# Splitting the weights of an encoder trunk into two float32r parts by DMAs of GpSimd instead of by VectorE

## The chip, the cores and the metric

One core of a Trainium2 chip runs the whole program. The metric is the device time of one execution in microseconds (us). The engines are named as in the profile: PE (TensorE matmuls), PEld (its weight loads), DVE (VectorE), ACT (ScalarE), POOL (GpSimd) and SP (SyncE, which here only issues DMAs).

## The reference

Two layers of an encoder over 512 tokens of width 1024, in float32. Each layer has a token mixer and a gated MLP, each between two RMS norms and added to the residual:

```python
for l in range(DEPTH):
    xn = rms_norm(x, norm_pre_mix[l])
    mix = mixer_layer(xn, w_in[l], w_out[l], ...)
    x = x + rms_norm(mix, norm_post_mix[l])
    xn = rms_norm(x, norm_pre_ffn[l])
    ff = conv_ffn(xn, w_up[l], conv_w[l], conv_b[l], w_down[l])
    x = x + rms_norm(ff, norm_post_ffn[l])
```

The mixer projects `xn` by `w_in` (1024 x 3584) into the inputs of three mixers, dilated window attention (A), a gated linear recurrence (B) and differential attention (C), and projects their outputs by `w_out` (1024 x 1024). `conv_ffn` projects to 2 x 2816 columns (`w_up`), mixes each column over three neighbouring tokens, multiplies `silu(gate) * val`, and projects back (`w_down`).

## The kernel before, in words

**Two-part products.** TensorE works on float32r, a float32 with a rounded mantissa. To keep float32's accuracy, an operand `a` of the large projections is kept as a rounded part `hi` and a rest `lo = a - hi`, both float32r, and a product is three matmuls: hi x hi, hi x lo, lo x hi (`prod`). So each weight tile is needed in both parts.

**Weight tiles.** `lay_weights` cuts all weights of a layer into 104 tiles of 128 partitions x 1024 float32 (512 KB). The tiles of `hg0` and `hg1` use only 768 columns (384 KB). `weight` (line 518) records what loads and splits a tile: SP loads it into `raw` (3 buffers), a copy rounds it into `hi`, and VectorE subtracts, `lo = raw - hi`. `hi` and `lo` have 5 buffers each (`WB`, line 1182), plus one pair for the last tile of a layer's MLP (`V_TILE`). The copy may go to VectorE or to ScalarE, as the planner decides (`copy`, line 241). In all 228 tiles are loaded: the 208 of two layers and, once more, the 6 tiles of `hg0` and `ib` and the first 4 of the MLP in each layer, because those projections run over half of the tokens at a time.

**Stages of a layer.** The norm transposes `xn` to the feature-major layout. `mixer` runs its projections and attention pieces in the order of `STEPS` (line 111), first `hg0` and `ib` twice over 256 tokens each (matmuls of 256 columns). Of an `hg0` tile such a half uses 18 matmuls (2 k-tiles, 3 outputs, 3 products), of an `ib` tile 24. Then come the output projection (first halves of the columns for all tokens, then second halves token block by token block, with four tiles held), and the MLP. The MLP starts with two column groups over 256 tokens at a time, 8 tile loads with 24 matmuls of 256 columns each; after that an up tile is used by 24 matmuls of 512 columns, and so is a down tile. For the last three pairs of down tiles all six tiles are held and the four token blocks run through them, six matmuls of 512 columns for each tile and token block.

**What sets the order.** The program is recorded op by op, and `Plan.order` (line 334) decides the order on every engine by a list schedule over estimated costs: each engine in turn takes the ready op of the lowest priority number. `weight` records its ops 1500 places ahead (`AHEAD`, line 109), so that a weight is loaded as soon as a buffer is free. A buffer is free when its last reader is done. The engines then execute these orders strictly, each waiting on semaphores. In that schedule a DMA issued by SP costs 1 ns for 350 bytes, and whoever needs its data comes 2000 ns later (`LAG["dma"]`). Besides SP's loads there are few other queues: GpSimd does 24 + 16 `memset`s and 48 power instructions (`pow`, the reciprocal roots of the norms; `row_rstd` and `rstd`), and no DMA. Everything that the planner issues has one line in the profile, L499.

## Time and profile before

| what | value |
|---|---|
| median of 3 runs | 1433.16 us (1432.78 to 1433.42) |
| the profiled execution's own time | 1432.73 us |
| its span, first to last instruction | 1431.0 us |
| TensorE matmuls, busy | 1391.2 us, 97% |
| VectorE, busy | 1051.7 us, 73% |
| ScalarE, busy | 656.6 us, 46% |
| GpSimd, busy | 56.7 us, 4% |
| mean granted TensorE clock | 0.999 |
| read from HBM | 128.4 MB, 93 GB/s over the span with what is written |

Busy time of an engine counts its instructions, not its waits. A row of the table of stretches gives, for each engine, the busy microseconds in it and the number of instructions, then the granted clock of TensorE (1.00 is full), the mean busy share of the core's 16 DMA engines, and what they moved. In groups of instructions, `128x1024 fp32r<-128x1024 f32` is the shape and type written and read, `x204` the count, then come the total busy time, the mean of one in ns, and the idle time of that engine just before these instructions with what ended it. `rounded` is the arena of float32r buffers (`hi` and `lo` parts), `full` that of float32 buffers, `w_d` the weights in HBM, `bank` a PSUM bank.

### The profile page before, as it was taken

What the parts mean: (1) busy time and instruction counts of PE and PEld (TensorE: products, weight loads), DVE (VectorE), ACT (ScalarE), POOL (GpSimd) and SP (SyncE); (2) the same over time, 40 slices, a digit from 0 to 9 for tenths busy, and PEclk for the clock granted to TensorE, in tenths of its full rate; (3) what the DMA queues carried; (4) which work ended last, traced back from release to release, by engine and by line L of the source; (5) the groups of instructions that cost most, each with busy time, mean ns of one, the idle gap of its engine ahead of it and who ended that gap; (6) DMA issues with size and microseconds to landing.
All of it is one profiled execution on the core that took longest, in us unless ns stands there. A gap on an engine that the chain in (4) does not pass through costs nothing.

```text
span 1431.0 us, 20879 instructions
## 1 busy us (share of the span) xinstructions
PE 1391.2 (97%) x8128; PEld 1208.8 (84%) x8128; DVE 1051.7 (73%) x1905; ACT 656.6 (46%) x1201; POOL 56.7 (4%) x94
## 2 busy tenths in 40 slices
PE   6999999999999999999999999999999999999998
PEld 6998888978888888888899888898788888888886
DVE  7779999886976546655777899888688765565574
ACT  5746886564533122213367478856555321321131
POOL 2000000001000000000010000000010000000000
PEclk9999999999999999999999999999999999999999
DMA  7412111221632223232262121012224223222321
GB/s 257 140 66 76 49 42 33 75 88 60 198 101 100 99 93 103 89 103 89 77 217 90 62 77 41 31 63 89 74 88 163 94 97 103 89 103 90 102 74 59
DMA packets 39363, 133.92 MB, mean 94 GB/s; under 512 B 5088, under 2 KB 5600, under 8 KB 39264
## 3 DMA queue, kind: packets, MB, share of 16 engines
q1 hardware_dynamic: 39264, 132.59, 27.5%
q8 instruction: 64, 1.05, 0.3%
q14 instruction: 35, 0.29, 0.1%
HBM read 128.37 MB, written 4.19 MB: 93 GB/s over the span
## 4 chain that ended last, share of the span: by engine, by line
PE 75%; DVE 17%; ACT 3%; issue 3%; DMA 1%; POOL 0%; DVEq 0%; SPq 0%; POOLq 0%; ACTq 0%
PE bank L499 75%; DVE full L499 10%; DVE rounded L499 6%; DVE qz L499 2%; ACT full L499 1%; ACT rounded L499 1%; DMA full<-w_d 1%; POOL full L499 0%; ACT L499 0%; DMA full<-x_d 0%; SPq L499 0%; DVEq L1245 0%; DVE masks L499 0%; POOLq L1245 0%; DVEq L499 0%
## 5 line engine op out<-in xcount | busy, mean ns | idle before, releaser
L499 PE MATMUL bank<-rounded 128*128 128x512 f32 (+1 forms) x6480 | 1234.5, 347 | 6.0 <-ACT full L499 2.0
L499 PEld LDWEIGHTS bank<-rounded 128*128 128x128 f32 x6480 | 1032.2, 190 | 153.5 <-DVE full L499 4.3
L499 DVE TENSOR_TENSOR rounded<-full,rounded 128x1024 fp32r<-128x1024 f32 (+2 forms) x276 | 302.0, 1106 | 50.9 <-ACT rounded L499 43.1
L499 ACT ACTIVATE rounded<-full 128x1024 fp32r<-128x1024 f32 (+2 forms) x162 | 152.8, 947 | 234.8 <-PE bank L499 182.7
L499 ACT ACTIVATE full<-bank,full 128x512 f32<-128x512 f32 (+1 forms) x184 | 122.7, 671 | 276.4 <-PE bank L499 243.0
L499 ACT ACTIVATE full<-full 128x512 f32<-128x512 f32 (+7 forms) x302 | 167.9, 572 | 168.0 <-DVE full L499 155.4
L499 DVE CAST rounded<-full 128x1024 fp32r<-128x1024 f32 (+1 forms) x114 | 74.2, 651 | 153.4 <-PE bank L499 147.5
L499 DVE SCALAR_TENSOR_TENSOR full<-bank,full 128x511 f32<-128x511 f32 x176 | 130.4, 748 | 55.4 <-ACT full L499 52.7
L499 DVE TENSOR_TENSOR full<-full 128x512 f32<-128x512 f32 (+2 forms) x277 | 145.7, 545 | 9.5 <-ACT full L499 3.2
L499 ACT ACTIVATE full<-bank 128x512 f32<-128x512 f32 (+3 forms) x188 | 103.2, 562 | 49.4 <-PE bank L499 37.1
L499 PE MATMUL bank<-ident,full 128*128 128x128 f32 x560 | 90.0, 281 | 18.9 <-DVE full L499 18.5
L499 PEld LDWEIGHTS bank<-ident,full 128*128 128x128 f32 x560 | 65.7, 143 | 33.8 <-DVE full L499 23.5
L499 PE MATMUL bank<-full 128*128 128x128 f32 (+2 forms) x640 | 83.5, 299 | 2.2 <-ACT full L499 1.4
L499 PEld LDWEIGHTS bank<-full 128*128 128x128 f32 (+1 forms) x640 | 70.6, 180 | 13.5 <-ACT full L499 5.0
L499 DVE SCALAR_TENSOR_TENSOR full<-full 128x512 f32<-128x512 f32 x96 | 69.6, 747 | 11.0 <-POOL full L499 10.4
L499 ACT ACTIVATE rounded<-bank 64x256 fp32r<-64x256 f32 (+1 forms) x148 | 63.3, 430 | 28.2 <-PE bank L499 21.0
L499 PE MATMUL bank<-qz,full 128*128 128x128 f32 x448 | 66.0, 288 | 5.8 <-DVE full L499 5.6
L499 POOL TENSOR_TENSOR full<-full,half 128x1 f32<-128x1 f32 (+1 forms) x48 | 42.1, 878 | 719.0 <-DVE full L499 719.0
L499 PEld LDWEIGHTS bank<-qz,full 128*128 128x128 f32 x448 | 56.1, 190 | 14.0 <-DVE full L499 11.9
L499 DVE TENSOR_TENSOR full<-bank,full 128x512 f32<-128x512 f32 (+1 forms) x56 | 35.9, 649 | 21.8 <-PE bank L499 21.5
L499 DVE TENSOR_TENSOR qz<-full 64x256 f32<-64x256 f32 x112 | 46.6, 416 | 4.4 <-PE bank L499 2.5
L499 DVE TENSOR_TENSOR rounded<-bank,rounded 64x256 fp32r<-64x256 f32 (+1 forms) x84 | 44.3, 535 | 5.4 <-ACT rounded L499 4.5
(54 smaller groups left out, 365.0 us busy)
## 6 DMA issues: line engine op xcount, KB each, us to landing
full<-w_d SPq DMA_DIRECT2D x204, 512.0 KB, 3.3
full<-w_d SPq DMA_DIRECT2D x24, 384.0 KB, 3.4
full<-x_d SPq DMA_DIRECT2D x8, 512.0 KB, 5.0
full<-gains_d SPq DMA_DIRECT2D x8, 512.0 KB, 4.1
spill<-full SPq DMA_DIRECT2D x4, 512.0 KB, 2.7
full<-spill SPq DMA_DIRECT2D x4, 512.0 KB, 4.2
out_d<-full SPq DMA_DIRECT2D x8, 256.0 KB, 2.0
abias<-abias_d SPq DMA_DIRECT2D x1, 448.0 KB, 7.1
```

What stands on the lines that cost most here:

```text
L499: f(*[real(v) for v in op.args], **{k: real(v) for k, v in op.kw.items()})
```

## The change

From the ninth tile on, a weight is no longer loaded raw. GpSimd issues a DMA from HBM straight into `hi`, whose type is float32r, so that the DMA rounds; a copy writes `lo = -hi` (on VectorE or ScalarE); and a second DMA of GpSimd reads the same weights from HBM once more and adds them to `lo`. The first 8 tiles (6 of 768 columns, 2 of 1024) are loaded and split as before. The planner's estimates follow: a DMA issued by GpSimd keeps GpSimd for 1000 ns (`SOFT`), and the lag of 2000 ns holds for every DMA.

```diff
+SOFT = 1000.0
+FIRST = 8
...
-        if op.eng == "gpsimd":
+        if op.eng == "gpsimd" and op.method != "dma_start":
...
-        lag = lambda a, b: LAG["dma"] if a.eng == "sync" else LAG[a.eng] if a.eng == b.eng else LAG["other"]
+        lag = lambda a, b: LAG["dma"] if a.method == "dma_start" else LAG[a.eng] if a.eng == b.eng else LAG["other"]
...
-            if e == "sync":
-                free[e] = max(t + 50, t + op.cost)
-                op.end = t + op.cost
+            if op.method == "dma_start":
+                issue = 50 if e == "sync" else SOFT
+                free[e] = max(t + issue, t + op.cost * (e == "sync"))
+                op.end = t + issue * (e != "sync") + op.cost
...
         with nc.ahead(AHEAD):
-            raw = self.t([128, n], "raw")
-            nc.sync.dma_start(raw, self.a["w"][l, index, :, 0:n])
+            src = self.a["w"][l, index, :, 0:n]
+            self.loads += 1
+            if self.loads <= FIRST:
+                raw = self.t([128, n], "raw")
+                nc.sync.dma_start(raw, src)
             hi = self.t([128, n], tag + "hi", F32R)
-            nc.copy(hi, raw)
+            if self.loads <= FIRST:
+                nc.copy(hi, raw)
+            else:
+                nc.gpsimd.dma_start(hi, src)
             lo = self.t([128, n], tag + "lo", F32R)
-            nc.vector.tensor_tensor(lo, raw, hi.bitcast(F32), op=ALU.subtract)
+            if self.loads <= FIRST:
+                nc.vector.tensor_tensor(lo, raw, hi.bitcast(F32), op=ALU.subtract)
+            else:
+                nc.copy(lo, hi.bitcast(F32), -1.0)
+                nc.gpsimd.dma_start(lo, src, accum_op=ALU.add)
         return hi, lo
```

Since the planner sorts anew, the order changes on every engine. Two places on GpSimd and one on VectorE follow. A row names the line, the operation, what it writes and reads, and in brackets the semaphores that it waits for: of the DMAs, those that wait for `PE` are rounding DMAs (a `hi` buffer has to be free), those that wait for `DVE` or `Activation` are adding DMAs (the negated copy has to be there). `DMASW0` to `DMASW7` are the semaphores of GpSimd's DMAs: each DMA also waits for the one eight places before it.

GpSimd from the output projection to the start of the MLP in layer 0; `full<-full,half` are the power instructions of the norms. Before:

```order
L499 TENSOR_TENSOR full<-full,half 128x4 [waits DVE_49,Activation_49,Pool_49]
L499 TENSOR_TENSOR full<-full,half 128x1 [waits DVE_49] x7
L499 TENSOR_TENSOR full<-full,half 128x1 [waits DVE_49,Pool_49]
L499 MEMSET full 64x4 [waits DVE_49,Activation_49]
```

Now:

```order
L502 TENSOR_TENSOR full<-full,half 128x1 [waits DVE_49]
L502 DMA rounded<-w_d 128x1024 [waits DMASW1_49,DVE_49]
L502 TENSOR_TENSOR full<-full,half 128x1 [waits DVE_49] x3
L502 DMA rounded<-w_d 128x1024 [waits DMASW2_49,PE_49]
L502 TENSOR_TENSOR full<-full,half 128x1 [waits DVE_49]
L502 DMA rounded<-w_d 128x1024 [waits DMASW3_49,PE_49]
L502 DMA rounded<-w_d 128x1024 [waits DMASW4_49,PE_49]
L502 DMA rounded<-w_d 128x1024 [waits DMASW6_49,DMASW5_49,PE_49]
L502 DMA rounded<-w_d 128x1024 [waits Activation_49]
L502 TENSOR_TENSOR full<-full,half 128x1 [waits DVE_49]
L502 DMA rounded<-w_d 128x1024 [waits DMASW7_49,DVE_49]
```

The power instructions, which stood in a row, now stand behind DMAs that wait for buffers and for negated copies.

GpSimd inside the MLP of layer 0, where it had nothing to do before (the loads were a run on SP, `L499 DMA full<-w_d 128x1024 x61`). Now:

```order
L502 DMA rounded<-w_d 128x1024 [waits DMASW2_49,PE_49]
L502 DMA rounded<-w_d 128x1024 [waits DMASW3_49,PE_49]
L502 DMA rounded<-w_d 128x1024 [waits DMASW4_49,DVE_49]
L502 DMA rounded<-w_d 128x1024 [waits DMASW5_49,PE_49]
L502 DMA rounded<-w_d 128x1024 [waits DMASW6_49,Activation_49]
L502 DMA rounded<-w_d 128x1024 [waits DMASW7_49,PE_49,Activation_49]
```

Rounding and adding DMAs alternate in one queue: two that wait for TensorE, then an adding one, and the next rounding one behind it.

VectorE in the MLP of layer 0: the taps of the convolution (`SCALAR_TENSOR_TENSOR`), the product with the gate, the split of its result (128x512), and of the weights (128x1024). Before:

```order
L499 CAST rounded<-full 128x512
L499 TENSOR_TENSOR rounded<-full,rounded 128x512 x2
L499 TENSOR_TENSOR rounded<-full,rounded 128x1024
L499 CAST rounded<-full 128x1024
L499 TENSOR_TENSOR rounded<-full,rounded 128x1024
L499 SCALAR_TENSOR_TENSOR full<-bank_66,full 128x511 x2
L499 CAST rounded<-full 128x1024
L499 TENSOR_TENSOR rounded<-full,rounded 128x1024
```

Now:

```order
L502 SCALAR_TENSOR_TENSOR full<-bank_66,full 128x511 x2
L502 TENSOR_TENSOR full<-full 128x512
L502 TENSOR_SCALAR rounded<-rounded 128x1024 x2
L502 SCALAR_TENSOR_TENSOR full<-bank_65,full 128x511 x2
L502 SCALAR_TENSOR_TENSOR full<-bank_63,full 128x511 x2
L502 TENSOR_TENSOR full<-full 128x512
L502 TENSOR_SCALAR rounded<-rounded 128x1024 x2
```

The subtractions of 1024 columns are gone; negating copies (`TENSOR_SCALAR`) stand where rounding copies (`CAST`) stood. Over the program GpSimd now issues 440 DMAs, SP 220 loads fewer.

## Rows read from the trace of the kernel before

**Rows 1.** The page's head: busy time, share of the span, instructions of each engine.

```profile
span 1431.0 us, 20879 instructions
...
PE 1391.2 (97%) x8128; PEld 1208.8 (84%) x8128; DVE 1051.7 (73%) x1905; ACT 656.6 (46%) x1201; POOL 56.7 (4%) x94
```

**Rows 2.** Table of stretches (starts of layers and MLPs, mixers, inner MLP).

```profile
core 0: us, PE busy (x) PEld busy (x) DVE busy (x) ACT busy (x) POOL busy (x), PEclk, DMA share, GB/s
29.00:58.00 29.00, 29.00 (x244) 29.00 (x243) 21.85 (x41) 22.23 (x32) 0.00 (x0) 1.00 0.58 195
100.00:200.00 100.00, 96.16 (x690) 85.70 (x689) 93.33 (x238) 73.89 (x134) 3.70 (x8) 1.00 0.16 54
200.00:300.00 100.00, 97.96 (x717) 88.31 (x715) 89.97 (x217) 65.99 (x152) 5.77 (x8) 1.00 0.21 70
371.00:394.00 23.00, 23.00 (x145) 20.95 (x146) 20.52 (x26) 12.96 (x17) 0.00 (x0) 1.00 0.60 200
500.00:600.00 100.00, 100.00 (x442) 82.75 (x441) 57.94 (x73) 25.74 (x36) 0.00 (x0) 1.00 0.29 100
724.00:753.00 29.00, 27.66 (x232) 27.46 (x232) 21.59 (x28) 19.53 (x30) 2.64 (x4) 1.00 0.65 217
800.00:900.00 100.00, 95.90 (x686) 86.27 (x687) 94.69 (x243) 74.20 (x134) 3.37 (x7) 1.00 0.16 54
900.00:1000.00 100.00, 97.88 (x726) 87.95 (x725) 88.66 (x215) 66.08 (x150) 6.11 (x8) 1.00 0.20 65
1075.00:1098.00 23.00, 22.68 (x144) 20.58 (x144) 20.36 (x26) 13.46 (x17) 0.00 (x0) 1.00 0.58 189
```

**Rows 3.** Waits, whole span: who waited for whom; us in total, times, longest.

```profile
PEld bank L499 <- DVE full L499: 42.6, 75, 7.3
...
PE bank L499 <- DVE full L499: 26.2, 36, 7.3
ACT rounded L499 <- DMA full<-w_d: 16.2, 13, 4.2
```

**Rows 4.** Groups of instructions, each shape apart: subtractions and rounding copies of weights.

```profile
L499 DVE TENSOR_TENSOR rounded<-full,rounded 128x1024 fp32r<-128x1024 f32 x204 | 249.3, 1223 | 32.8 <-ACT rounded L499 25.1 <-DVE rounded L499 0.5
...
L499 ACT ACTIVATE rounded<-full 128x1024 fp32r<-128x1024 f32 x108 | 114.1, 1058 | 89.5 <-PE bank L499 77.5 <-DMA full<-w_d 11.9
...
L499 DVE CAST rounded<-full 128x1024 fp32r<-128x1024 f32 x96 | 66.5, 693 | 121.5 <-PE bank L499 115.7 <-DMA full<-w_d 1.6
...
L499 DVE TENSOR_TENSOR rounded<-full,rounded 128x768 fp32r<-128x768 f32 x24 | 22.7, 951 | 9.7 <-ACT rounded L499 9.7
...
L499 ACT ACTIVATE rounded<-full 128x768 fp32r<-128x768 f32 x24 | 20.2, 843 | 26.1 <-PE bank L499 21.6 <-DMA full<-w_d 4.3
```

**Rows 5.** DMA queue and issues (KB each, median us to landing); SP's issue of weights.

```profile
q1 hardware_dynamic: 39264, 132.59, 27.5%
...
full<-w_d SPq DMA_DIRECT2D x204, 512.0 KB, 3.3
full<-w_d SPq DMA_DIRECT2D x24, 384.0 KB, 3.4
full<-x_d SPq DMA_DIRECT2D x8, 512.0 KB, 5.0
...
L499 SPq DMA_DIRECT2D full<-w_d x228: 327/328/600, 3.1 to 1383.2; - x114
...
DMA to landing us min/median/max: 2.8/3.3/9.1
```

**Rows 6.** Groups of instructions: GpSimd's power instruction of the norms.

```profile
L499 POOL TENSOR_TENSOR full<-full,half 128x1 f32<-128x1 f32 x32 | 26.0, 812 | 464.8 <-DVE full L499 464.8
```

**Rows 7.** TensorE in order of time, start of layer 0: start, length, operation.

```profile
14.64 2.73 PE L499 MATMUL bank<-rounded 128*128 128x256 f32 x12
...
29.01 41.16 PE L499 MATMUL bank<-rounded 128*128 128x256 f32 x341
```

More of the change, by code (lines that the diff above doesn't have):

```diff
@@ L504, in __init__ @@
         self.nc, self.const, self.a = plan, const, a
+        self.loads = 0
     def t(self, shape, tag, dt=F32):
```

## The prediction

> **What bounds the kernel now.** I read the page's head first [rows 1]: TensorE is busy for 97% of the span, VectorE for 73%, GpSimd for 4%. So the question is not how much VectorE work goes, but where TensorE stands still for VectorE. The table of stretches [rows 2] answers that. Through the gated MLP TensorE is busy without a gap (500 to 600 us: 442 matmuls, 226 ns each), while VectorE is at 58%: nothing can be won there. TensorE has gaps only in the two token-mixing stages, where VectorE is at 89 to 95%: 3.84 and 2.04 us in layer 0, 4.10 and 2.12 us in layer 1, 12.1 us in all. The waits say the same [rows 3]: TensorE's two rows on VectorE come to 68.8 us, but they count weight loads beside matmuls, and only gaps in the matmul column move the end. Weights are hardly waited for: 16.2 us of ScalarE's time, none of TensorE's.
>
> The same table shows where the DMAs are dense: at the starts of the layers and of the MLPs 256-column matmuls use up a weight tile in half the time, and there the 16 DMA engines are busy for 58 to 65% of the stretch, against 29% inside the MLP.
>
> **The change, part by part.** The sum is made against the profiled execution, 1432.7 us, 0.4 us under the median of the runs.
>
> *VectorE loses its subtractions.* Of 228 tiles the first 8 (6 of 768 columns, 2 of 1024) stay as they were. That leaves 202 subtractions of 1.223 us and 18 of 0.951 us, 264 us of VectorE's time [rows 4]. The 220 rounding copies go too, but 220 negating copies of the same size replace them, on either engine. By the order of instructions 119 wide copies of 1.058 us and 21 of 0.843 us now stand on ScalarE, against 108 and 24 before: 9 us more on an engine that is 46% busy, nothing. Of the 264 us most lies beside a TensorE that never waited. What can come back is the 12.1 us of gaps. In layer 0's two stretches the DMAs move 54 and 70 GB/s, 12.4 MB or some 24 tiles, so 29 us of VectorE's 183 us there are subtractions. That is a sixth, so the chains of the mixers stay, and I take half of the gaps: **6 us gained**, between 0 and 12.
>
> *One plain load becomes two DMAs on GpSimd's queue.* A plain 512 KB load occupies the 16 engines for 27.5% x 1431.0 us x 0.524 MB / 132.59 MB = 1.56 us and lands 3.3 us after its issue [rows 5]. The rounding DMA moves as many bytes; I price it as a plain load. The adding DMA has no row. Lower bound: it costs a plain load too, 1.56 us. Nearer to what it must do is 3.11 us, two plain loads, since both the weights and the negated tile have to be read; I take this. For the upper end both DMAs are half as fast again or more (6.2 us for the pair), which no row excludes. So a 1024-column tile asks for 4.67 us of all engines (3.11 to 6.2), a 768-column one for 3.50 us. The Trainium skill ("Collectives: The Full Stack", the section on the bandwidth ceiling) says that an add in the DMA engines is slow not for the arithmetic but because it needs two source reads, and gives a ratio of 1.93; by it the pair would be an estimated 4.57 us and the sum below 3 us lower. No run here has shown an adding DMA yet.
>
> Against that stands what TensorE takes for a tile. Inside the MLP: 24 matmuls of 226 ns, 5.43 us. So 4.67 us fits (86% of the engines), no loss. In the 256-column places a matmul takes 119 ns (29 to 58 us, 244 of them) [rows 2]: an up tile or half an ib tile 24 of them, 2.85 us; an hg0 tile 18, 2.14 us. There the DMAs now bound:
> - both MLP starts, 8 tiles each: 2 x 8 x (4.67 - 2.85) = 29.1 us;
> - start of layer 1: 8 x (3.50 - 2.14) + 4 x (4.67 - 2.85) = 18.2 us;
> - the last four tiles of layer 0's start: 2 x 1.36 + 2 x 1.82 = 6.4 us.
>
> Together **53.7 us**. Tiles that are loaded before a place begins take off at most one 4.67 us each; the first tile's chain (next point) adds as much, and I let them cancel.
>
> *A tile is ready later.* Before, raw tiles lie ready, and a free slot costs a copy and a subtraction. Now a slot that comes free starts a chain: rounding DMA 3.3 us, negation 0.69 to 1.06 us (nearest rows, the rounding copies [rows 4]), adding DMA 3.3 us and 1.56 us more for the second read. GpSimd's issue has no row; between SP's 0.33 us [rows 5] and the 0.81 us of GpSimd's power instruction [rows 6] I take the former, as it is an issue too, twice. That makes 9.5 to 9.9 us, 9.7 in the middle; with a cheap addition and the shorter negation 7.95 us at the least. In the MLP five slots give 4 x 5.43 = 21.7 us: covered. At the end of each projection, where tokens go through tiles that are all held, six matmuls (1.36 us) lie between the tiles, and the last slot has 5 x 1.36 = 6.8 us. Short by 2.9 us, at two ends in each of two layers: **11.6 us** (4.6 at the least).
>
> *GpSimd's queue.* 440 DMAs now stand in it, in order. Behind an adding DMA that waits for its negation stand the next rounding DMA and, at the norms, the power instruction that VectorE waits for next (the first order rows of the section on the change). In layer 0's MLP each rounding DMA stands behind the addition of a tile ahead of it. The chain's first half, 0.33 + 3.3 + 1.06 = 4.69 us, is less than a tile's 5.43 us, so this costs nothing; the cover is gone when that half takes 0.7 us longer. SP's queue loses 220 loads, and residual rows and gains are no longer behind weights: nothing, they were not waited for.
>
> Sum: 1432.7 + 53.7 + 11.6 - 6 = **1492 us**.
>
> **The rivals.**
>
> *The adding DMA is cheap (faster).* At 3.11 us for the pair the dense places lose 2 x 8 x 0.26 + 8 x 0.19 + 4 x 0.26 + 0.9 = 7.6 us, which one or two tiles loaded ahead at each place take back; the four ends lose 4.6 us. With 6 to 12 us of the gaps won back that gives 1425 to 1431 us, say **1427**. It decides at a pair of about 3.4 us. For it: the engines are idle for 71% of the MLP. Against it: the bytes. Chance 0.22.
>
> *The MLP gives way too.* If the pair costs more than 5.43 us, or the DMAs land late enough that GpSimd's queue alternates without slack, each of 2 x (66 - 14) = 104 inner tiles is late. At 6.2 us: 104 x 0.79 = 82 us, and the dense places grow to 2 x 8 x 3.37 + 8 x 2.54 + 4 x 3.37 + 12 = 100 us; with 11.6 lost at the ends and 6 won that is **1620 us**. For it: landings of up to 9.1 us exist, and loads that run four at a time (the x rows) take 5.0 us instead of 3.3 [rows 5]. Against it: the inner MLP has 14% of slack in my price. Chance 0.20.
>
> *VectorE's copies hold up GpSimd's descriptors.* A 1024-column rounding copy on VectorE takes 0.69 us, little over half of a subtraction's 1.22 us [rows 4]. If such an instruction kept GpSimd from preparing a DMA, each of a tile's two issues could be late by 0.69 us, at the four ends 4 x 1.4 = 5.6 us: **1498 us**, inside my range. The Trainium skill ("SBUF — State Buffer", "SBUF: two separate sides") states this as a trap for DMAs issued from GpSimd; no row here shows it, since GpSimd issues none yet. Chance 0.05.
>
> *The gaps and the losses cancel*, or the pair of DMAs rounds and adds in the time of one load and the order alone changes little: 1433, chance 0.11.
>
> **How the numbers follow.** My own case has 0.42, the cheap addition 0.22, the MLP's giving way 0.20, the held descriptors 0.05, no change 0.11. My case alone spans 1455 (half of the dense loss) to 1540 (first tiles late as well, and a slow restart of TensorE: after its early stall the same 256-column matmuls took 228 ns each, 2.73 us for 12, against 121 ns later [rows 7]). The range must take in the cheap addition and part of the MLP case: 1422 to 1610; beyond it lie the dearer half of the MLP case and little below. Faster and slower mean by over 0.2%, about what a measurement of this kernel can tell from no change: 0.22 faster, 0.11 within, 0.67 slower.
>
> **What would show it.** Right: the DMA share at the MLP starts and at layer 1's start near 1, TensorE with gaps there that wait for a DMA; inside the MLP TensorE without gaps and a DMA share near 0.86; mixing stages with VectorE at some 80% and smaller gaps; the adding DMA landing about 5 us after issue. Wrong: a DMA share near 0.6 inside the MLP (the addition is cheap), or TensorE waiting for weights inside the MLP (the pair costs over 5.4 us, or GpSimd's order binds).

## The result, and the profile after

The changed kernel takes **1524.46 us** (median of 4 runs, 1521.94 to 1527.33) against 1432.97 us for the kernel before on the same chip: ratio **1.064, 95% interval 1.062 to 1.066**, 91.5 us slower. The profiled execution spans 1525.6 us, 94.6 us more than before.

First the page's head, and its part on the DMA queues (packets, MB, share of 16 engines):

```profile
span 1525.6 us, 20987 instructions
...
PE 1421.4 (93%) x8128; PEld 1233.3 (81%) x8128; DVE 806.8 (53%) x1687; ACT 651.6 (43%) x1195; POOL 374.3 (25%) x534
...
q0 software_dynamic: 63360, 226.00, 65.6%
q1 hardware_dynamic: 7584, 19.59, 3.7%
```

The DMA issues (KB each, median us to landing), and the two groups of instructions that took the place of the subtractions (busy us, mean ns of one, idle time of the engine before them):

```profile
rounded<-w_d POOLq DMA_DIRECT2D x404, 512.0 KB, 5.9
```
```profile
L502 POOL DMA_DIRECT2D rounded<-w_d x440 | 322.4, 785 | 949.5 <-PE bank L502 384.7 <-ACT rounded L502 278.7 <-DVE rounded L502 247.7
L502 DVE TENSOR_SCALAR rounded<-rounded 128x1024 fp32r<-128x1024 f32 (+1 forms) x87 | 60.5, 695 | 316.1 <-DMA rounded<-w_d 279.5 <-PE bank L502 23.9 <-issue 12.6
```

VectorE is relieved by 245 us, from 73% to 53% [rows 1], and the kernel is slower: VectorE was not the bound. The price is in the queue of GpSimd's DMAs: 65.6% of 1525.6 us for 226.00 MB, so the two DMAs of a 512 KB tile (1.049 MB) take 1000.8 x 1.049 / 226.00 = **4.64 us** of the 16 engines, where the one plain load took 1.56 [rows 5].

The table of stretches, with the columns of [rows 2]: a mixing stretch of layer 0, start of its MLP, inside the MLP, start of layer 1, a mixing stretch of layer 1, inside its MLP.

```profile
200.00:300.00 100.00, 97.63 (x745) 87.89 (x742) 79.26 (x219) 66.59 (x149) 17.04 (x23) 1.00 0.36 86
390.00:420.00 30.00, 25.38 (x135) 22.04 (x135) 12.66 (x18) 9.29 (x12) 9.57 (x14) 0.94 0.94 223
420.00:540.00 120.00, 120.00 (x531) 99.40 (x530) 42.08 (x58) 41.31 (x54) 31.56 (x45) 1.00 0.89 197
...
760.00:815.00 55.00, 39.23 (x259) 37.10 (x258) 16.69 (x29) 23.91 (x39) 24.85 (x33) 0.84 1.01 243
870.00:970.00 100.00, 95.56 (x681) 85.03 (x679) 87.38 (x243) 74.42 (x145) 18.89 (x26) 1.00 0.48 103
...
1170.00:1300.00 130.00, 130.00 (x575) 107.66 (x574) 44.17 (x61) 41.47 (x55) 34.06 (x48) 1.00 0.88 193
```

Read the DMA share, the last column but one. At the starts it is 0.94 to 1.01 and TensorE has gaps; the start of layer 1 runs 259 matmuls in 55 us, where 29 us held 232 before [rows 2]. Inside the MLPs it is 0.88 to 0.89 and TensorE has no gap in these stretches. In the mixers VectorE went from 90% to 79% (200 to 300 us), and TensorE is no busier than before: 97.63 us of 100 against 97.96.

The waits (total us, times, longest):

```profile
DVE rounded L502 <- DMA rounded<-w_d: 279.5, 70, 15.4
...
ACT rounded L502 <- DMA rounded<-w_d: 204.9, 84, 7.1
...
PE bank L502 <- DMA rounded<-w_d: 46.4, 24, 5.0
...
PE bank L502 <- DVE full L502: 40.9, 25, 7.4
```

TensorE now waits for weights, 46.4 us in 24 places, which it never did. But its waits for VectorE have grown too, from 26.2 us [rows 3] to 40.9. The growth is not where VectorE is busy: four of these waits, 3.42, 5.40, 4.69 and 5.86 us, 19.4 in all, stand inside the MLPs, where TensorE had no gap before. This is TensorE, ScalarE, GpSimd and VectorE in order of time in layer 0's MLP:

```profile
549.17 0.90 POOL L502 DMA_DIRECT2D rounded<-w_d  x1
...
552.85 0.55 POOL L502 DMA_DIRECT2D rounded<-w_d  x1 [2.78 <-PE bank L502]
556.30 1.06 ACT L502 ACTIVATE rounded<-rounded 128x1024 fp32r<-128x1024 f32 x1 [3.99 <-DMA rounded<-w_d]
557.26 1.43 ACT L502 ACTIVATE full<-bank,full 128x512 f32<-128x512 f32 x2
557.65 0.87 POOL L502 DMA_DIRECT2D rounded<-w_d  x1 [4.25 <-ACT rounded L502]
558.05 2.73 DVE L502 SCALAR_TENSOR_TENSOR full<-bank,full 128x511 f32<-128x511 f32 x4 [4.07 <-ACT full L502]
...
560.28 2.23 PE L502 MATMUL bank<-rounded 128*128 128x512 f32 x7 [3.42 <-DVE full L502]
```

ScalarE stands for 3.99 us at a negation whose rounding DMA has not landed. That is the DMA of the first row, issued at 549.17; the one at 552.85 is the next tile's. The profile's view of it names who waited, and the time to its landing:

```profile
  ACT rounded L502: 4.0, 1
...
DMA to landing us min/median/max: 7.1/7.1/7.1
```

Behind the negation in ScalarE's order are the two instructions of the gate, whose last matmuls had ended by 544.39. VectorE's taps wait for them (4.07 us), the PSUM banks stay occupied, and TensorE stops for 3.42 us. The DMA itself was issued late: by the order of the program the last matmul that read its `hi` buffer ended at 546.88, and until 549.17 it stood in GpSimd's queue behind the additions of the two tiles before it. There are four such places, where TensorE goes on at 560, 698, 1317 and 1456 us. At each of them ScalarE stands at a negation (3.99, 5.96, 5.25 and 6.43 us); its rounding DMA left GpSimd 2.3 to 4.7 us after its buffer was free and landed 7.1, 6.7, 7.6 and 7.7 us after that.

To see where the 94.6 us arise, the start of the first matmul that reads a given weight tile is compared in both traces, and the same for two of the experiments below. (TensorE's matmuls are matched with tiles by their order in the program.) A column holds by how many us that matmul comes later than in the kernel before:

| where (tile) | before at | after | e2, later landing planned | e11, no second DMA |
|---|---|---|---|---|
| start of layer 0 over (first gb tile) | 72.6 | 10.1 | 10.0 | 1.4 |
| mixers over (last tile of output projection) | 332.0 | 12.0 | 4.6 | 0.4 |
| MLP start over (8th up tile) | 398.5 | 23.3 | 19.3 | -0.8 |
| inner MLP over (first of the last six down tiles) | 686.9 | 35.9 | 19.3 | -0.9 |
| start of layer 1 over (gb) | 777.1 | 62.6 | 48.6 | 0.2 |
| mixers over | 1036.4 | 64.0 | 45.3 | -1.3 |
| MLP start over | 1102.9 | 74.5 | 59.1 | -3.0 |
| inner MLP over | 1391.3 | 89.5 | 59.3 | -3.0 |
| end of the span | 1431.0 | 94.6 | 60.1 | -1.4 |

The differences of neighbouring rows are the stages' losses. After the change: starts and ends of projections 10.1 + 11.3 + 26.7 + 10.5 + 5.1 = 63.7 us, mixers 1.9 + 1.4 = 3.3 us, inside the MLPs 12.6 + 15.0 = 27.6 us.

Not all of this is standing still. TensorE needs 1421.4 us for the 8128 matmuls that took 1391.2 before [rows 1], at a mean granted clock of 0.975 instead of 0.999: of the 94.6 us 64.4 are gaps and 30.2 are slower matmuls. Of the 27.6 us inside the MLPs 19.4 are the four gaps and 8.2 the slower matmuls behind them. At the starts, where TensorE waits for DMAs anyway, slower matmuls also fill time that would have been gaps; how much they add there was not separated.

### The profile page after: what moved, and what is told of

Its sections match the earlier page's. It is cut to its first block, busy times and chain, and to the rows that moved or that the text cites. A ratio compares the mean times of both kernels' runs of the same rounds, so it can differ in the third digit from the quotient of the medians.

```text
span 1525.6 us, 20987 instructions
## 1 busy us (share of the span) xinstructions
PE 1421.4 (93%) x8128; PEld 1233.3 (81%) x8128; DVE 806.8 (53%) x1687; ACT 651.6 (43%) x1195; POOL 374.3 (25%) x534
## 3 DMA queue, kind: packets, MB, share of 16 engines
q0 software_dynamic: 63360, 226.00, 65.6%
## 4 chain that ended last, share of the span: by engine, by line
PE 37%; issue 29%; DVE 11%; POOL 11%; DMA 8%; ACT 2%; POOLq 0%; DVEq 0%; SPq 0%; ACTq 0%
PE bank L502 37%; POOL rounded L502 10%; DVE full L502 8%; DMA rounded<-w_d 7%; DVE rounded L502 2%; DVE qz L502 1%; ACT rounded L502 1%; POOL full L502 1%; ACT full L502 1%; DMA full<-x_d 0%; DMA full<-w_d 0%; POOLq L502 0%; ACT L502 0%; SPq L502 0%; DVEq L1261 0%
## 5 line engine op out<-in xcount | busy, mean ns | idle before, releaser
L502 PE MATMUL bank<-rounded 128*128 128x512 f32 (+1 forms) x6480 | 1266.1, 353 | 73.5 <-DMA rounded<-w_d 46.4
L502 PEld LDWEIGHTS bank<-rounded 128*128 128x128 f32 x6480 | 1052.8, 194 | 231.1 <-DMA rounded<-w_d 53.5
L502 POOL DMA_DIRECT2D rounded<-w_d x440 | 322.4, 785 | 949.5 <-PE bank L502 384.7
L502 DVE TENSOR_SCALAR rounded<-rounded 128x1024 fp32r<-128x1024 f32 (+1 forms) x87 | 60.5, 695 | 316.1 <-DMA rounded<-w_d 279.5
L502 ACT ACTIVATE rounded<-rounded 128x1024 fp32r<-128x1024 f32 (+1 forms) x133 | 137.4, 1034 | 208.5 <-DMA rounded<-w_d 204.9
L502 ACT ACTIVATE full<-full 128x512 f32<-128x512 f32 (+6 forms) x300 | 167.6, 573 | 99.1 <-DVE full L502 89.0
L502 DVE TENSOR_TENSOR full<-full 128x256 f32<-128x256 f32 (+2 forms) x277 | 145.8, 545 | 11.1 <-POOL full L502 3.6
L502 ACT ACTIVATE full<-bank 128x512 f32<-128x512 f32 (+3 forms) x163 | 90.2, 565 | 97.6 <-PE bank L502 74.3
L502 PEld LDWEIGHTS bank<-ident,full 128*128 128x128 f32 x560 | 68.2, 146 | 27.6 <-DVE full L502 16.4
L502 ACT ACTIVATE rounded<-full 128x512 fp32r<-128x512 f32 (+2 forms) x46 | 31.1, 677 | 113.9 <-PE bank L502 75.1
L502 PEld LDWEIGHTS bank<-full 128*128 128x128 f32 (+1 forms) x640 | 71.2, 180 | 10.5 <-ACT full L502 3.7
L502 DVE TENSOR_TENSOR rounded<-full,rounded 128x512 fp32r<-128x512 f32 (+2 forms) x56 | 40.6, 738 | 24.5 <-ACT rounded L502 21.8
```

What stands on the lines that cost most here:

```text
L502: f(*[real(v) for v in op.args], **{k: real(v) for k, v in op.kw.items()})
```

## The experiments

Theory: a stage loses what the DMA engines need for a tile beyond what TensorE needs for it; inside the MLP the loss is one of order, ScalarE held at a negation whose DMA lands late. Rivals: the type conversion is dear, not the addition; latency and GpSimd's queue cost, not engine time; VectorE's copies hold up GpSimd's DMAs.

### The price of a tile: no addition, no second DMA, a third DMA

**e1**, the second DMA loads instead of adding:

```diff
-                nc.gpsimd.dma_start(lo, src, accum_op=ALU.add)
+                nc.gpsimd.dma_start(lo, src)
```

> The second DMA of a tile no longer adds: it loads the weights once more, rounded, over the negated copy. So the addition is left out and lo holds the rounded weights; everything else (two DMAs per tile in GpSimd's queue, the negation, the order) stays. Theory (the adding DMA occupies the engines twice as long as a rounding one, and engine time is what the dense places pay): the queue's time per pair of DMAs falls from 4.64 to about 3.1 us, TensorE needs 2.85 or 2.14 us for a tile there, so of some 45 us lost at the dense places about 8 remain, and the ends get back some 6 us as the second landing is shorter: 1475 to 1490 us; if the VectorE stalls inside the MLP hang on late DMAs too, down to 1455. Rival A (the type conversion is what costs, in both DMAs alike): the pair stays at 4.6 us and the time at 1520 to 1528. Rival B (latency and the order in GpSimd's queue, not engine time): the pair falls to 3.1 us but the time stays above 1510.

Measured: 1454.7 us, ratio 1.016 (1.014 to 1.018). The queue, and GpSimd's issues:

```profile
q0 software_dynamic: 63360, 226.00, 49.2%
```
```profile
L502 POOL DMA_DIRECT2D rounded<-w_d x440 | 235.7, 537 | 954.5 <-PE bank L502 570.1 <-ACT rounded L502 216.5 <-DVE rounded L502 144.3
```

49.2% of 1453.0 us for the same bytes is 3.32 us for a pair, 1.66 us for a rounding DMA. So the adding one took 4.64 - 1.66 = **2.98 us**, and the conversion costs next to nothing (1.66 against 1.56): rival A falls. The time lands at the lower end of what was expected, and the stalls inside the MLP are gone with it: DMAs that land earlier relieve ScalarE as well. But the price does not tell where the rest is lost. At 3.32 us a pair it accounts for 1.6 us at the start of layer 0 and 4.7 at that of layer 1; by the comparison of tiles 8.5 and 12.3 us are lost there, and 2.8 and 0.5 at the two MLP starts, where it would be 3.8 each.

**e11**, the second DMA is left out altogether (the last line of the same diff is deleted and none added).

> The adding DMA is left out: lo stays the negated rounded part, so the second load and the addition are missing from the computation. The rest of the change stands as it was, with the planner's 1000 ns. It is the third point of a row: a tile costs the DMA engines 4.64 us in the full change (1524 us), 3.31 us with a plain second load (1455 us), and here 1.66 us, less than TensorE's 2.14 us for a tile. Theory (engine time): no loss is left at the dense places, what remains is the longer chain of rounding DMA and negation: 1430 to 1440 us. Rival (GpSimd's queue or the negation that waits for a DMA costs by itself): 1445 to 1460.

Measured: **1431.43 us, ratio 1.000 (0.999 to 1.001)**. So GpSimd's queue with 220 rounding DMAs and negations that wait for them costs nothing by itself; the rival falls as far as half of the queue can show it. And it shows what VectorE's relief is worth:

```profile
PE 1388.6 (97%) x8128; PEld 1210.2 (85%) x8128; DVE 816.9 (57%) x1692; ACT 645.2 (45%) x1190; POOL 173.0 (12%) x314
```

VectorE has 235 us less to do than before [rows 1], no DMA is late at the starts, and the kernel is not faster. In the table above this run gains 1.0 and 1.5 us in the mixers, and loses 1.6 us at the end again. TensorE's gaps there are not smaller. From the first gb tile to the first tile of the output projection, and from there to its last tile, before and in this run (layer 0):

```profile
72.60:286.50 213.90, 207.50 (x1555) 189.09 (x1554) 191.19 (x479) 144.96 (x292) 8.46 (x14) 1.00 0.17 57
286.50:332.00 45.50, 43.63 (x240) 35.40 (x240) 32.25 (x62) 24.32 (x56) 4.06 (x5) 1.00 0.26 92
```
```profile
74.00:287.50 213.50, 207.02 (x1555) 188.89 (x1554) 172.02 (x458) 142.07 (x294) 22.02 (x37) 1.00 0.19 56
287.50:332.30 44.80, 42.83 (x239) 35.40 (x239) 29.29 (x59) 23.03 (x52) 4.70 (x7) 1.00 0.27 90
```

VectorE does 19 us less in the long stretch, and TensorE's gaps are 6.40 us before and 6.48 now; in the output projection they are 1.87 and 1.97.

**e12**, one load more for each tile, with the planner's estimate of e2 below:

```diff
+                nc.gpsimd.dma_start(lo, src)
                 nc.copy(lo, hi.bitcast(F32), -1.0)
```

> The full change with the planner's 2300 ns (1493 us), and one more load per tile: a third DMA of GpSimd writes the rounded weights into lo beside the one into hi, before the negation overwrites it. The result stays the same; a tile now costs the DMA engines 4.64 + 1.66 = 6.30 us, more than the 5.43 us that TensorE takes for it inside the MLP. Theory (engine time of a tile against TensorE's time for it, in each stage): the DMA share goes to 1.0 inside the MLP, where TensorE waits now, 104 tiles x 0.87 us = 90 us, and the dense places lose 49 us more (16 x 1.66 + 8 x 1.24 + 4 x 1.66 + 5.8): 1632 us, 1600 to 1660. Rival (the losses hang on the length of the chain and on GpSimd's order, which five slots cover inside the MLP): no gaps there, 1495 to 1560.

Measured: 1684.22 us, ratio 1.177 (1.175 to 1.180). Two stretches inside the MLPs:

```profile
440.00:600.00 160.00, 147.46 (x630) 118.03 (x629) 54.09 (x77) 38.33 (x53) 50.94 (x78) 0.99 0.98 264
1420.00:1600.00 180.00, 163.50 (x693) 130.84 (x691) 56.88 (x82) 35.28 (x51) 56.41 (x87) 0.98 0.96 250
```

Now the MLP is bound by the DMAs as well: share 0.98 and 0.96, and 630 matmuls in 160 us make 6.10 us for a tile's 24, where they took 5.43. The queue's 77.5% of 1681.6 us for 338.99 MB is 6.05 us a tile. The mechanism holds, and against the rival; the sum does not, and the time lies 24 us above its range. By the comparison of tiles this run is 190.4 us later than e2 at its end: 86 us of that are lost inside the MLPs (90 expected), 59 at starts and ends (49 expected), and 45 in the mixers, where nothing was expected. Why the mixers lose was not tried. (The inner tiles are 2 x (40 + 16) = 112, not 104: 8 loads at an MLP's start are 4 tiles, loaded twice.)

### The stalls inside the MLP: the planner's estimate

**e2**:

```diff
-SOFT = 1000.0
+SOFT = 2300.0
```

> Only the planner's estimate changes: a DMA of GpSimd keeps the queue for 2300 ns instead of 1000, which is half of the 4.64 us that a pair of DMAs occupies the engines, so it expects a landing 5.8 us after issue, near the measured median of 5.9. Theory (inside the MLP a negation stands in ScalarE's order ahead of the gate's two instructions and waits for a rounding DMA; VectorE's taps and then TensorE's next banks wait behind it; four such places cost about 27 us): with honest estimates the negations are put behind the gate, the four stalls shrink or go, 1495 to 1510 us, the dense places as before. Rival (the DMAs are late whatever the order, so the wait only moves to another instruction): 1518 to 1530 us. A planner that expects later landings can also order the first half of a chain worse at the dense places: then slower than 1530.

Measured: **1493.13 us, ratio 1.043 (1.041 to 1.044)**: 31 us back from one number of the planner, slightly more than expected. Same DMAs, same bytes, but another order on every engine; inside the MLP there is no gap any more, and at the start of the MLP (first row) the DMAs bind as in the full change:

```profile
385.00:412.00 27.00, 24.09 (x131) 21.33 (x131) 12.42 (x19) 8.86 (x11) 7.95 (x11) 0.87 0.98 237
412.00:540.00 128.00, 128.00 (x567) 106.01 (x566) 53.54 (x75) 27.08 (x39) 35.03 (x48) 1.00 0.93 198
540.00:690.00 150.00, 150.00 (x663) 123.96 (x662) 60.29 (x86) 33.90 (x48) 39.45 (x55) 1.00 0.90 192
```

So the 27.6 us were a matter of the order, ScalarE's at the four places, and not of the DMAs' capacity. What is left, 60.1 us, is 68.6 us at starts and ends and 0.2 inside the MLPs, less 8.7 us that the mixers won back. Where the start is not late, they win little or nothing (e11; e5 and e6 below). 6.5 of the 8.7 us lie in the output projections; in layer 0:

```profile
294.40:336.60 42.20, 42.20 (x240) 35.68 (x239) 28.89 (x60) 23.39 (x52) 9.82 (x13) 1.00 0.58 147
```

TensorE has no gap there, where it had 1.87 us before and 1.97 in e11 with the same work on VectorE (28.89 and 29.29 us). In e11 ScalarE waits in this stretch for 4.1 us at negations. So less work on VectorE alone does not close these gaps; whether it does once ScalarE is not held, or whether the mixers' chains ran on while TensorE waited for weights, was not separated.

### Where it is lost: the old path at some places

**e3** keeps the old path for the tiles of the dense places and of the ends, **e4** for all but the mixers' tiles; **e5** and **e6** are the same two with e2's 2300 ns. In `weight`, for e3 and e5:

```diff
+DENSE = set([*range(BASE["hg0"], BASE["hg0"] + 4), *range(BASE["ib"], BASE["ib"] + 2),
+             *range(BASE["out"], BASE["up"] + 4), *range(BASE["down"] + 16, BASE["down"] + 22)])
...
+            old = self.loads <= FIRST or index in DENSE
-            if self.loads <= FIRST:
+            if old:
```

For e4 and e6 the second line of the set runs from `BASE["out"]` to `BASE["down"] + 22`.

> The weights of the dense places and of the projections' ends (hg0, ib, the output projection, the first four up tiles, the last six down tiles) are loaded by SP and split as before the change; all others, 160 of 228 tiles, by GpSimd's pair of DMAs. Theory (dense places about 45 us and ends about 17 us are lost there and nowhere else, the stalls inside the MLP, about 27 us, are a separate loss by the order on ScalarE): 1433 + 27 + 0 to 4 = 1455 to 1470 us, DMA share at the MLP starts back at 0.6 to 0.7, no TensorE wait for weights there. Rival (a stream of paired DMAs upsets GpSimd's queue and the engines' orders everywhere, and the dense places only show it): above 1485 us. If the stalls inside the MLP come from DMAs still late from the start of the MLP, they go too: 1433 to 1440 us.

> Only the tiles that the mixers use after the start of a layer (24 per layer, where VectorE is busy for 90 to 95% and the DMA engines for 16 to 20%) come by GpSimd's pair of DMAs; all others as before the change. VectorE loses about 29 us of subtractions in each layer just there. Theory of the prediction (half of the mixers' 12.1 us of gaps comes back): 1427 us, 1421 to 1433. Rival (the mixers' chains do not hang on VectorE's load, and the power instructions and negations behind waiting DMAs cost as much; the full change showed 2 to 4 us more there): 1433 to 1440 us.

> Both edits of the last four runs together: the dense places and the ends by the old path (that alone gave 1470 us), and the planner's 2300 ns for a DMA of GpSimd (that alone gave 1493). Theory (three separate losses: engine time at the dense places, order inside the MLP, waits for DMAs in the mixers): the stalls inside the MLP, 23 us in the first of the two, go: 1440 to 1448 us; if the mixers' waits go with the order too, 1433 to 1438. Rival (the stalls inside the MLP come from the DMAs' load and only changed place): above 1458 us.

> Only the mixers' 24 tiles per layer by GpSimd's pair (that alone gave 1445 us, 14 us over before), with the planner's 2300 ns. Theory (in the mixers VectorE and ScalarE stand in order behind a negation whose rounding DMA has not landed, 2.0 us in one place seen, and TensorE's operands behind them): with later estimates most of this goes, 1430 to 1438 us. Rival A (VectorE's relief then shows as well, the prediction's half of the gaps): 1421 to 1429. Rival B (what is lost is where the new path sets in, at the start of the mixers, where the pair comes later than the raw tile did, whatever the order): 1441 to 1448.

Measured: e3 1470.11 us (ratio 1.026, 1.024 to 1.028), e4 1445.46 (1.010, 1.008 to 1.011), e5 1440.87 (1.007, 1.005 to 1.009), e6 1439.49 (1.005, 1.004 to 1.007).

e3 lies at the upper edge of its range: the stalls inside the MLP are still there (by the comparison of tiles 4.7, 9.9, 1.6 and 7.2 us, 23.4 in all), and of the 63.7 us of the dense places and ends some 9 are left. With 2300 ns (e5) the stalls go, and e5 is within 1.4 us of e6: 112 inner tiles by GpSimd's pair cost nothing once the order is right. The losses inside the MLP and at the dense places are separate, as the theory says.

The mixers miss the prediction. e4 is 14 us over before, where 6 us less had been expected, and above its rival's range too. A place in its trace, VectorE, GpSimd and TensorE in order of time:

```profile
131.09 0.87 POOL L502 DMA_DIRECT2D rounded<-w_d  x1
...
138.79 0.69 DVE L502 TENSOR_SCALAR rounded<-rounded 128x1024 fp32r<-128x1024 f32 x1 [2.00 <-DMA rounded<-w_d]
...
139.40 1.37 DVE L502 COPY full<-bank 64x512 f32<-64x512 f32 x2
...
142.40 0.87 PEld L502 LDWEIGHTS bank<-qz,full 128*128 128x128 f32 x5 [2.35 <-DVE full L502]
142.40 0.95 PE L502 MATMUL bank<-qz,full 128*128 128x128 f32 x4 [2.15 <-DVE full L502]
```

It is the MLP's stall again, on VectorE: 2.00 us at a negation that waits for its DMA, issued at 131.09 and landed 7.6 us later, the mixers' own copies behind it, TensorE 2.15 us late. With a later landing planned (e6) that goes, and 8 us remain over before, between the theory's range and that of rival B. Its table of stretches, two mixing stretches and the two places where the pair sets in behind the dense start of a layer:

```profile
100.00:200.00 100.00, 96.06 (x694) 86.75 (x694) 87.94 (x238) 72.33 (x144) 19.00 (x28) 1.00 0.48 104
200.00:300.00 100.00, 97.65 (x714) 87.30 (x711) 84.43 (x206) 61.45 (x138) 9.71 (x13) 1.00 0.29 81
```
```profile
30.00:60.00 30.00, 28.05 (x222) 27.85 (x221) 18.76 (x45) 21.27 (x29) 6.40 (x9) 0.94 0.81 227
740.00:770.00 30.00, 27.71 (x219) 27.51 (x218) 19.27 (x37) 22.55 (x33) 6.77 (x9) 0.94 0.85 224
```

The same two places before:

```profile
30.00:60.00 30.00, 30.00 (x252) 30.00 (x251) 23.00 (x44) 23.29 (x36) 0.10 (x1) 1.00 0.53 181
740.00:770.00 30.00, 30.00 (x253) 30.00 (x251) 23.75 (x34) 25.40 (x39) 0.10 (x1) 1.00 0.44 145
```

In the mixers VectorE is at 88 and 84% instead of 93 and 90%, and TensorE at 96.06 and 97.65 us instead of 96.16 and 97.96 [rows 2]: the relief is not seen. What e6 loses, it loses for the most part in the two places behind the dense starts (5.1 us by the comparison of tiles): 28.05 and 27.71 us of TensorE, 30.00 in both stretches before, at a granted clock of 0.94. **e9** spares these places: only hg1, qkc0 to qkc3 and vc0, vc1, the mixers' late tiles, come by the pair.

> Only the tiles that the mixers use late (hg1, qkc0 to qkc3, vc0 and vc1, 16 per layer) by GpSimd's pair, with the planner's 2300 ns; the tiles that follow the dense start of a layer (va, qka0, gb, qka1) by the old path again. Theory (what the mixers-only kernel lost, 8 us, was lost at the two places where the pair sets in right behind the dense start, a stall of about 2 us each and 4 to 6 us of TensorE at a lower granted clock; VectorE's relief itself brings nothing, since TensorE's gaps in the mixers hang on chains): 1430 to 1434 us. Rival A (the relief is worth the prediction's 3 to 6 us once the start is spared): 1424 to 1428. Rival B (each place where the pair sets in costs a stall): 1436 to 1442.

Measured: 1434.33 us, ratio 1.0025 (1.0017 to 1.0034). This is 0.3 us above the theory's range: the loss at the starts is gone (at most 0.7 us by the comparison of tiles), nothing is won, and 3.1 us remain, about half of them behind the last matmul. No kernel of this study is faster than the one before.

### Half of the change, six slots, negations on one engine

**e8** rounds by GpSimd's DMA and keeps SP's raw load and the subtraction:

```diff
-                nc.copy(lo, hi.bitcast(F32), -1.0)
-                nc.gpsimd.dma_start(lo, src, accum_op=ALU.add)
+            nc.vector.tensor_tensor(lo, raw, hi.bitcast(F32), op=ALU.subtract)
```

> Half of the change: from the ninth tile on GpSimd's DMA rounds into hi, but SP loads the raw tile as before and VectorE subtracts; no negation and no adding DMA. A tile then costs the engines a plain load and a rounding one, 1.56 + 1.66 = 3.2 us, against TensorE's 2.85 or 2.14 us at the dense places; VectorE keeps 264 us of subtractions and loses the rounding copies. Theory (engine time of the adding DMA and the wait for negations made the loss): the dense places lose 2 x 8 x 0.4 + 8 x 1.1 + 4 x 0.4 + 3 = 20 us at most, half of that with tiles ahead: 1440 to 1455 us, no stalls inside the MLP. Rival (any instruction of VectorE that waits for a DMA of GpSimd upsets the mixers and the MLP, as subtractions now do): 1460 to 1480 us.

Measured: 1451.66 us, ratio 1.013 (1.011 to 1.015), inside the theory's range. e1, with 3.32 us a tile, came out alike (1454.7 us), but the places differ: by the comparison of tiles e1 loses 20.8 us at the starts of the layers and 3.3 at those of the MLPs, this run 5.3 and 7.5. So the price of a tile alone does not decide; what makes the difference between the places was not tried.

**e7** has a sixth pair of buffers:

```diff
-WB = 5
+WB = 6
...
-    base = place(fa, fsize, 0, (("raw", 4 * K, 3), ("sm", 4, 16)))
+    base = place(fa, fsize, 0, (("raw", 4 * K, 1), ("sm", 4, 16)))
```

> The full change with the planner's 2300 ns (1493 us) and six pairs of buffers for hi and lo instead of five; the room comes from the raw buffers, one instead of three, which only the first 8 tiles use. Theory (dense places hang on engine time, ends on the chain's length): the dense places get one tile more ahead, up to 4.6 us each at three places, the four ends 1.4 us or more each; the first tiles of layer 0 lose 2 to 6 us to the single raw buffer: 1470 to 1488 us. Rival A (latency limits the dense places as well, so that a sixth tile in flight raises their rate by a fifth): 1455 to 1470. Rival B (engine time alone, the ends too): 1490 to 1497.

Measured: 1493.67 us, ratio 1.043 (1.041 to 1.045), as e2. The test is blunt: by the comparison of tiles the single raw buffer costs 12 us at the start of layer 0 (22.4 us late against 10.0), not 2 to 6, and later stages win some 10 us back, about 5 of them at each MLP start. The time misses the theory's range and lies in that of rival B. A rate limited by latency would have won more; since the single raw buffer cost more than was allowed for, the run does not decide between the theory and rival B.

**e10**, every negation on ScalarE, with 2300 ns:

```diff
-                nc.copy(lo, hi.bitcast(F32), -1.0)
+                nc.scalar.activation(lo, hi.bitcast(F32), AF.Copy, scale=-1.0)
```

> The full change with the planner's 2300 ns (1493 us), but every negation on ScalarE: VectorE does no copy of a weight any more, 59 us or more less work. Theory (VectorE's copies do not hold up GpSimd's DMAs, and VectorE's time is not what the losses hang on): 1488 to 1498 us, with mean issue time of GpSimd's DMAs unchanged, near 0.76 us. Rival (the prediction's held descriptors, 1.4 us at each of four ends): 1482 to 1487 and a shorter mean issue. Another (ScalarE, with 220 negations of 1.06 us each waiting for a DMA, holds up the gate inside the MLP): above 1500.

Measured: 1494.87 us, ratio 1.045 (1.043 to 1.047), against e2's 1.043 (1.041 to 1.044): no gain. Issues of GpSimd's DMAs take 740 ns in the mean, in e2 762:

```profile
L502 POOL DMA_DIRECT2D rounded<-w_d x440 | 314.2, 740 | 945.4 <-PE bank L502 579.9 <-ACT rounded L502 319.8 <-ACT full L502 24.5
```

Taking VectorE's copies of weights away shortens an issue by 22 ns. The rival of the held descriptors needs 0.69 us per issue. The Trainium skill ("SBUF — State Buffer", "SBUF: two separate sides") describes such a lock; here it is not seen at a size that matters, though VectorE still had other copies in this kernel.

## Why the prediction was right, and where not

The forecast was 1492 us in a range of 1422 to 1610; measured were 1524.46. Direction and main cause hold; one loss of 27.6 us was put at nothing, and it is most of the difference. Without it, in e2, the time is 1493 us. That this meets the forecast to 1 us is luck in part: by place the losses at starts and ends differ from the forecast and cancel, and the 8.7 us that the mixers win back in e2 lie for the most part in the output projections, not in the gaps that the forecast counted.

- **Price of the pair: right.** 4.67 us were taken, 4.64 measured; the parts were 1.56 + 3.11 and are 1.66 + 2.98. The reason taken was that the adding DMA reads two sources for every byte written; the price fits it, but no run shows the reads. The ratio of the Trainium skill ("Collectives: The Full Stack", the section on the bandwidth ceiling) gave an estimate of 4.57 us; the trace agrees within 2% for the pair.
- **Dense places and ends: right in sum, by luck in part.** 53.7 + 11.6 = 65.3 us forecast, 63.7 measured, 68.6 with the better order (e2). By place the sizes shift: start of layer 0 10.1 instead of 6.4, end of the MLP and start of layer 1 26.7 instead of 21.1, end of the output projection and start of the MLP 11.3 and 10.5 instead of 17.5 each. So the starts of the layers lose more than forecast and those of the MLPs less, and the two cancel. Tiles loaded ahead before the MLP starts would explain the one; that was not tried (e7 is blunt). At the start of layer 1 TensorE restarts slowly, 259 matmuls in 39.23 us of busy time (151 ns each, 119 before [rows 2]) at a granted clock of 0.84. That engine time is not all at the starts of the layers e1 shows, with 20.8 us lost there where its price accounts for 6.3; what the rest is stays open.
- **Inside the MLP: capacity right, order wrong.** No gap for want of DMA time, share 0.86 forecast, 0.88 to 0.89 measured; e12 shows that a tile of 6.05 us does make the MLP give way, as the rival had it. The step that failed is "so this costs nothing" in the point on GpSimd's queue. It put the chain's first half at 4.69 us, with 3.3 us for the landing of the rounding DMA as for a plain load, and found that less than a tile's 5.43 us. At the stall shown above that half took 8.48 us, from the issue of the rounding DMA at 549.17 to that of the same tile's addition at 557.65, 7.1 us of it the landing; and before that the DMA stood 2.3 us in GpSimd's queue behind other tiles' additions. So the prediction's own condition, that the cover is gone when this half takes 0.7 us longer, was met there. Its rival of late landings named this, but with every inner tile late; it was four places. And the prediction did not ask what stands on ScalarE and VectorE behind a negation that waits for its rounding DMA. The raw tile was a buffer between the transfer and the engines; the negation has none, and with the order fixed a late landing becomes a late gate. e2 and e5 show that the order decides: the 27.6 us go by a planner's number alone. (The rival's 104 inner tiles are 112; its 82 us become 88.)
- **Mixers: wrong.** 6 us were to come back, 3.3 were lost. The step that failed is "I take half of the gaps", as if they hung on VectorE's load. e11 takes 235 us from VectorE and wins 2.5 us in the mixers, with TensorE's gaps as before (6.48 us against 6.40 up to the output projection of layer 0); e6 and e9 win none. So up to the output projection these gaps do not hang on how much work VectorE has; that they hang on chains of small dependent steps is the likely reading, and was not tried. In the output projection, 1.87 us a layer, e2 shows them closed, and why is open.
- **The chain and GpSimd's issue.** 0.33 us per issue were taken; measured are 0.54 us for a rounding DMA (e1) and 0.87 for an adding one (at 557.65). That this costs nothing e11 shows for the rounding DMAs alone.
- **The rivals.** The cheap addition falls by its price. Its forecast, 1427 us at 3.11 us a pair, would not have held either: at 3.32 (e1) the kernel was still 1.6% slower, and at 1.66 (e11) equal, not faster. In neither did gaps of the mixers come back that could have paid. The held descriptors fall as far as e10 reaches.

## What to carry to other kernels

Before moving work from an engine to the DMAs, compare the engines' time per tile with the consumer's time per tile in every stage, not on average: this pair cost nothing where a tile lasts 5.43 us, once the order was right, and bound the kernel where it lasts 2.1 to 2.9. When an instruction starts to wait for a transfer directly, look at what is queued behind it on its own engine, and give the planner the landing that the trace shows. And a busy engine in front of a gap is not yet the cause of the gap; taking 235 us of work from it and seeing the same time (e11) is the test.

## What the runs showed of the hardware

- A rounding DMA (float32 to float32r) of 512 KB takes the engines 1.66 us, hardly more than a plain load (1.56 [rows 5]); an adding one 2.98 us. The median landing of both kinds together was 5.9 us after issue, and 4.3 in e1:

```profile
rounded<-w_d POOLq DMA_DIRECT2D x404, 512.0 KB, 4.3
```

- The issue of an adding DMA stands in GpSimd's row for 0.87 us, that of a rounding one for 0.55 (the rows at 557.65 and 552.85). It does not keep the next issue back that long: behind the addition at 548.62 the rounding DMA's issue starts at 549.17, 0.55 us later.
- Around the stalls for weights the granted clock of TensorE is below full: 0.94 in the stretch at the MLP start and 0.84 at the start of layer 1, where stall followed stall. Inside the MLP, after the stop of 3.42 us that ends at 560.28, it falls to half, the lower of its two levels (1.2 and 2.4 GHz), and 6 matmuls of 512 columns take 2.00 us, 333 ns each instead of 226:

```profile
562.00:564.00 2.00, 2.00 (x6) 1.54 (x5) 1.56 (x3) 0.78 (x2) 0.00 (x0) 0.50 0.90 135
```

Part of what a late tile costs is paid in the matmuls after it: TensorE's busy time for the same 8128 matmuls is 30.2 us longer here.
